# An MoE block's weight splits, all on VectorE, and the gated product's transposes in another PSUM bank

## The chip, the cores and the metric

The kernel runs on one core of one Trainium2 chip. The metric is the device time of one execution in microseconds; where several executions were timed, their median. The engines are named as in the profile: PE is TensorE, with its weight loads as PEld; DVE is VectorE; ACT is ScalarE; POOL is GpSimd; SP is SyncE, which here only issues transfers. In the text they are also called TensorE, Vector, Scalar, Pool and SyncE.

## The reference

Three layers run over 512 tokens of width 1024 (and 256 context tokens in the first). Two of them mix attention, a Fourier and a long-convolution branch and have a convolutional feed-forward. The third is a dilated and a neighbourhood attention, followed by a mixture of experts and a last norm. The change lies in the mixture of experts alone:

```python
def hierarchical_moe(x, w_group, b_group, w_router, b_router, w_gate, w_up, w_down):
    '''Top-1 expert group, then top-2 SwiGLU experts inside it. x: (B,S,D).'''
    ...
    gate = jnp.einsum('nd,edf->nef', xf, w_gate)
    up = jnp.einsum('nd,edf->nef', xf, w_up)
    act = jax.nn.silu(gate) * up * combine[:, :, None].astype(x.dtype)
    out = jnp.einsum('nef,efd->nd', act, w_down)
    return out.reshape(B, S, D).astype(x.dtype)
```

There are 16 experts of width 256, and each of the 512 tokens goes to two of them.

## The kernel before

**Splits.** All data are float32. A matrix product is made of three products of fp32r parts: each operand is split into a high part (a copy in fp32r) and a low part (the original less the high part). `mm3` (lines 296 to 299) issues the three, high by high (L297), high by low (L298) and low by high (L299). For weights Scalar makes the high part (L2035) and Vector or Pool the low part (L2036), both in `wconv`. Both work on chunks of 128x1024.

**The routing** (`route`, from line 1863) sorts the tokens into tiles of 128 rows. Tiles 0 to 15 belong to one expert each, at places known when the kernel is written. Tiles 16, 17 and 18 hold the rows that did not fit; which expert's weights they need is known only on the chip, so their weights are gathered. If more are needed, a conditional part follows (four more tiles); it is not taken here.

**The tiles** run in the order 0 to 9, 16, 17, 18, 10 to 15 (`K.order`). By order of running they are counted 0 to 18 below where that is said. One tile, in `moe` (from line 2053), is:

- `load`: a gather of the tile's 128 rows (xg), issued on Pool two tiles ahead;
- `rows`: eight transposes of xg on TensorE into two PSUM banks (xgp, tag T), each split by Scalar and Vector (xgt, L327 and L328);
- `up`: 24 products of 128x512 from chunks 0 to 3 of the weights (gups), then silu on Scalar (L2080) and the gated product on Vector (ma, L2081);
- `act`: two transposes of ma on TensorE (mat, L2087) and their split (mas, L327 and L328). The bank of mat has the tag T, so it takes turns with the two of xgp;
- `down`: 12 products from chunks 4 and 5 (mdps), copied out by Scalar or Vector (yt) and stored from Scalar's queue. The last two tiles to run are kept in SBUF (yf) and scattered by a product with a matrix of zeros and ones (S).

`down` of a tile is issued behind `up` of the next one. After the fifth tile `scatter_from` builds S (fo, L1786, and its transposes fsp).

**The weights' stream.** `wstream` keeps 18 chunks (three tiles) loaded or under way: `wnext` takes a chunk, splits it and asks for the one 18 further on. Static chunks are loaded from SyncE's queue (L2015), gathered ones from Pool's (L2017). They go by turns into nine buffers called raw and into pages called rawp. A load waits until the splits of the buffer's earlier chunk are done, and the loads of a queue go in order.

**Which splits go to Pool.** `wnext` passes a flag: for static tiles, chunk 2 and chunk 5 (chunk 2 alone in the last tile, tile 15). These are 31 of the 118 splits that `wconv` makes (114 for the 19 tiles, four for the output projection ahead of the routing). Tiles 16 to 18 have all their splits on Vector.

**Order.** The instructions are ordered on each engine by a planner when the kernel is built. A semaphore wait holds up everything behind it on its engine.

**PSUM in this stage**: two banks each for the tags b (mdps), T (xgp, mat, fsp) and g (gups), one for r (the routing's logits and weights, rtp and rwsl) and one for r2.

Of the kernel before, what the change touches and what calls it, by code (L numbers as in the profile page):

```python
# [9 lines left out]
F32 = mybir.dt.float32  # L10
# [4 lines left out]
ALU = mybir.AluOpType  # L15
# [238 lines left out]
class Kern:  # L254
# [1485 lines left out]
    def second_tail(K, mix, xs):  # L1740
        nc, A = K.nc, K.A
# [15 lines left out]
            nc.scalar.dma_start(y[n * 128:n * 128 + 1, :], z)  # L1757
        lt = K.bank([128, 4, 20], name="rtp", tag="r")
        K.phase("wout2")
        ws = [K.wconv(t, False) for t in K.w2raw]  # L1760
        ro = K.branch_norm(1)
        K.wstream(5)
        for tb in range(4):
# [9 lines left out]
        T = {}  # L1773
# [44 lines left out]
        for tb in range(4):  # L1818
            t = ts[2 * tb + 1][0]
# [4 lines left out]
            for h in range(2):  # L1824
                ps = K.bank([128, 512], name="fsc", tag=("T", "g", "b", "T")[tb])
                c = slice(h * 512, h * 512 + 512)
# [6 lines left out]
        for tb in range(4):  # L1833
            ss = K.sm([128, 1], "fss")
            K.sumsq(xs[tb], ss)
            r = K.rsqrt(ss, 1, 1.0 / D, EPS, "fr")
# [188 lines left out]
            K.wq.append((c, j, K.wraw(j, c)))  # L2025
            K.wn += 1

    def wconv(K, raw, pool, pg=False):
        nc = K.nc
        if pg:  # L2030
            hi, lo = K.pg([128, 1024], F32R, "whx"), K.pg([128, 1024], F32R, "wlx")
        else:
            hi = K.wp.tile([128, 1024], F32R, tag="whi", name="whi", bufs=K.NW)
            lo = K.wp.tile([128, 1024], F32R, tag="wlo", name="wlo", bufs=K.NW)
        nc.scalar.activation(hi, raw, AF.Copy)  # L2035
        (nc.gpsimd if pool else nc.vector).tensor_tensor(lo, raw, hi.bitcast(F32), op=ALU.subtract)  # L2036
        return hi, lo

    def wnext(K, j, cs):
        out = []  # L2040
        for c in cs:
            c_, j_, raw = K.wq.popleft()
            assert (c_, j_) == (c, j)
            out.append(K.wconv(raw, j < 16 and c == (2 if j == K.order[-1] else 2 + 3 * (c > 3)), c > 3))
            K.wstream(K.WDEPTH)
        return out

# [5 lines left out]
    def moe(K, tiles, xnd, idx, wsl, weights=None, fin=(), T=None, mid=None, rest=None):  # L2053

        nc, A = K.nc, K.A
        if not weights:
            def weights(j, cs):
                return [K.wconv(K.wraw(j, c), False) for c in cs]

        def load(j):  # L2060
            x = K.page(j, "xg")
            nc.gpsimd.indirect_dma_start(out=x, out_offset=None, in_=xnd,
                                         in_offset=bass.IndirectOffsetOnAxis(ap=idx[:, j:j + 1], axis=0))
            return x

        def rows(x):
            t = [K.page(tiles[0], f"xgt{p}", F32R).rearrange("p (k n) -> p k n", n=128) for p in range(2)]
            for h in range(2):
                ps = K.bank([128, 4, 128], name="xgp", tag="T")
                for k in range(4):  # L2070
                    nc.tensor.transpose(ps[:, k], x[:, (4 * h + k) * 128:(4 * h + k) * 128 + 128], K.ident)  # L2071
                K.split(t[0][:, 4 * h:4 * h + 4], t[1][:, 4 * h:4 * h + 4], ps)
            return t

        def up(j, t, w):
            ps = K.bank([128, 512], name="gups", tag="g")
            for k in range(8):
                K.mm3(ps, (t[0][:, k], t[1][:, k]), (w[k // 2][0][:, k % 2], w[k // 2][1][:, k % 2]), k == 0, k == 7)
            a = K.t2([128, 256], "ma") if j < 19 else K.page(j, "ma")[:, 0:256]
            nc.scalar.activation(a, ps[:, 0:256], AF.Silu)  # L2080
            nc.vector.scalar_tensor_tensor(a, a, wsl[:, j:j + 1], ps[:, 256:512], op0=ALU.mult, op1=ALU.mult)  # L2081
            return a

        def act(a):
            pt = K.bank([128, 2, 128], name="mat", tag="T")
            for k in range(2):
                nc.tensor.transpose(pt[:, k], a[:, k * 128:k * 128 + 128], K.ident)  # L2087
            s = K.t2([128, 2, 2, 128], "mas", F32R)
            K.split(s[:, 0], s[:, 1], pt)
            return s  # L2090

        def down(j, s, w):
            if j in fin:
                T[fin.index(j)] = y = [K.pg([128, 1024], F32R, f"yf{p}") for p in range(2)]
            else:
                y = K.page(j, "yt")
            for h in range(2):
                c = slice(h * 512, h * 512 + 512)
                ps = K.bank([128, 512], name="mdps", tag="b")
                for k in range(2):  # L2100
                    K.mm3(ps, (s[:, 0, k], s[:, 1, k]), (w[k][0][:, c], w[k][1][:, c]), k == 0, k == 1)
                if j in fin:
                    K.split(y[0][:, c], y[1][:, c], ps)
                else:
                    K.ev(y[:, c], ps)
            if j not in fin:
                z, r = (0, j - 2 * (j > 15)) if j < 19 else (1, j - 19)
                nc.scalar.dma_start(K.yb[z][r * 128:r * 128 + 128, :], y)

        tiles = list(tiles)  # L2110
        xs = deque(load(j) for j in tiles[:2])
        t = rows(xs.popleft())
        prev = None
        for i, j in enumerate(tiles):
            if i + 2 < len(tiles):
                xs.append(load(tiles[i + 2]))
            w = [K.wk(v, 512) for v in weights(j, range(4))]
            a = up(j, t, w)
            if xs:
                t = rows(xs.popleft())  # L2120
            if prev:
                down(*prev)
            prev = (j, act(a), weights(j, (4, 5)))
            if mid and i == 4:
                mid()
        if rest:
            rest()
        down(*prev)
# [39 lines left out]
```

## Time and profile before

| | |
|---|---|
| median of three runs | 2298.61 us (2293.86 to 2303.5) |
| profiled execution | 2302.42 us, span 2300.6 us |
| PE busy | 2126.4 us, 92% of the span |
| DVE busy | 1472.3 us, 64% |
| ACT busy | 1013.4 us, 44% |
| POOL busy | 353.0 us, 15% |
| mean granted clock | 0.963 |

The shares are means over the whole span. The page's line of busy tenths in 40 slices shows that they differ by stage: in slices 37 to 39 Vector stands at 8 and 9 tenths, the DMA at 8 and 9, and Pool at 4 to 7, where it is at 0 to 3 in every slice before:

```profile
DVE  4644576567677777767558455565565645669895
ACT  3632562364332232236454464333344544347672
POOL 1300000011010000003100010000001112126744
PEclk8999999979999999998999989999999999979998
DMA  8352022723333344434120432333243345369893
```

One slice is 57.5 us; the experts' stage fills the last four to five. A row of the timeline gives the start in us from the span's start, the length in us, the engine, the line in the kernel, the operation, the tiles written and read, the shape, and in brackets how long the engine sat idle before and what ended that.

### The profile page before, as it was taken

What the parts mean: (1) busy time and instruction counts of PE and PEld (TensorE: products, weight loads), DVE (VectorE), ACT (ScalarE), POOL (GpSimd) and SP (SyncE); (2) the same over time, 40 slices, a digit from 0 to 9 for tenths busy, and PEclk for the clock granted to TensorE, in tenths of its full rate; (3) what the DMA queues carried; (4) which work ended last, traced back from release to release, by engine and by line L of the source; (5) the groups of instructions that cost most, each with busy time, mean ns of one, the idle gap of its engine ahead of it and who ended that gap; (6) DMA issues with size and microseconds to landing.
All of it is one profiled execution on the core that took longest, in us unless ns stands there. A gap on an engine that the chain in (4) does not pass through costs nothing. (4 is left out here: it accounts for less than half of the span.)

```text
span 2300.6 us, 30894 instructions
## 1 busy us (share of the span) xinstructions
PE 2126.4 (92%) x11802; PEld 1725.7 (75%) x11802; DVE 1472.3 (64%) x2451; ACT 1013.4 (44%) x1786; POOL 353.0 (15%) x331
## 2 busy tenths in 40 slices
PE   6999998989999999998998989999989998968895
PEld 3777677768888888886876778888867786756673
DVE  4644576567677777767558455565565645669895
ACT  3632562364332232236454464333344544347672
POOL 1300000011010000003100010000001112126744
PEclk8999999979999999998999989999999999979998
DMA  8352022723333344434120432333243345369893
GB/s 334 100 194 81 10 79 103 268 95 106 106 105 125 125 145 160 142 119 147 42 90 18 166 101 83 101 108 94 86 154 90 88 121 172 138 229 352 318 371 121
DMA packets 94394, 321.19 MB, mean 140 GB/s; under 512 B 11262, under 2 KB 12673, under 8 KB 94244
## 3 DMA queue, kind: packets, MB, share of 16 engines
q1 hardware_dynamic: 81472, 280.37, 35.2%
q0 software_dynamic: 10320, 29.89, 4.2%
q10 hardware_dynamic: 2452, 8.92, 1.0%
q8 instruction: 94, 1.54, 0.3%
q14 instruction: 56, 0.46, 0.1%
HBM read 279.39 MB, written 33.46 MB: 136 GB/s over the span
## 5 line engine op out<-in xcount | busy, mean ns | idle before, releaser
L318 DVE TENSOR_TENSOR wlo<-raw,whi 128x1024 fp32r<-128x1024 f32 x200 | 245.4, 1235 | 179.1 <-ACT whi L317 170.0
L317 ACT ACTIVATE whi<-raw 128x1024 fp32r<-128x1024 f32 x200 | 209.9, 1059 | 257.9 <-PE fps L298 194.3
L297 PE MATMUL fps<-h2x,whi 128*128 128x512 f32 x672 | 262.2, 391 | 3.8 <-DVE cvf L702 3.7
L298 PE MATMUL fps<-h2x,whi 128*128 128x512 f32 x672 | 262.5, 391 | 0.0
L299 PE MATMUL fps<-h2x,wlo 128*128 128x512 f32 x672 | 262.0, 391 | 0.0
L1295 DVE TENSOR_TENSOR y<-y,dps 128x512 f32<-128x512 f32 x200 | 134.0, 683 | 108.8 <-PE dps L299 104.1
L1372 POOL TENSOR_TENSOR cvf<-cvf 128x512 f32<-128x512 f32 x66 | 77.1, 1168 | 803.5 <-DVE cvf L702 703.2
L297 PEld LDWEIGHTS fps<-h2x,whi 128*128 128x128 f32 x672 | 126.3, 188 | 31.0 <-ACT whi L317 4.1
L700 ACT ACTIVATE cvf<-fps,cv 128x512 f32<-128x512 f32 (+1 forms) x126 | 87.5, 695 | 139.0 <-PE fps L299 138.9
L299 PEld LDWEIGHTS fps<-h2x,wlo 128*128 128x128 f32 x672 | 126.5, 188 | 27.7 <-issue 1.6
L298 PEld LDWEIGHTS fps<-h2x,whi 128*128 128x128 f32 x672 | 126.7, 188 | 25.8 <-issue 0.4
L298 PE MATMUL dps<-wlo,actx 128*128 128x512 f32 x352 | 137.1, 389 | 0.0
L297 PE MATMUL dps<-whi,actx 128*128 128x512 f32 x352 | 136.6, 390 | 0.3 <-DVE y L1295 0.3
L299 PE MATMUL dps<-whi,actx 128*128 128x512 f32 x352 | 136.6, 389 | 0.0
L420 DVE SCALAR_TENSOR_TENSOR ma<-wm,cs,ma 128x512 f32<-128x512 f32 x140 | 107.7, 814 | 17.4 <-DMA wm<-in_wmod 17.4
L297 PE MATMUL fps<-hx,whi 128*128 128x512 f32 x288 | 113.7, 395 | 0.5 <-ACT v L921 0.5
L299 PE MATMUL fps<-hx,wlo 128*128 128x512 f32 x288 | 113.3, 393 | 0.0
L298 PE MATMUL fps<-hx,whi 128*128 128x512 f32 x288 | 113.2, 393 | 0.0
L701 DVE SCALAR_TENSOR_TENSOR cvf<-fps,cv,cvf 128x511 f32<-128x511 f32 (+1 forms) x126 | 82.5, 655 | 30.2 <-ACT cvf L700 30.0
L297 PE MATMUL fps<-h2c,whi 128*128 128x256 f32 x336 | 96.3, 286 | 4.1 <-ACT cvf L700 4.1
L298 PE MATMUL fps<-h2c,whi 128*128 128x256 f32 x336 | 96.1, 286 | 0.0
L299 PE MATMUL fps<-h2c,wlo 128*128 128x256 f32 x336 | 96.1, 286 | 0.0
(579 smaller groups left out, 5250.3 us busy)
## 6 DMA issues: line engine op xcount, KB each, us to landing
wm<-in_wmod SPq DMA_DIRECT2D x96, 512.0 KB
raw<-in_wup SPq DMA_DIRECT2D x88, 512.0 KB
raw<-in_win SPq DMA_DIRECT2D x52, 512.0 KB
rawp<-in_wexp SPq DMA_DIRECT2D x48, 512.0 KB
raw<-in_wexp SPq DMA_DIRECT2D x48, 512.0 KB
raw<-in_wdown SPq DMA_DIRECT2D x44, 512.0 KB
raw<-in_wout SPq DMA_DIRECT2D x20, 512.0 KB
xd<-xt SPq DMA_DIRECT2D x20, 512.0 KB
```

The source lines that it names most:

```text
L297: mm(out, st[0], mv[0], start=start, stop=False)
L298: mm(out, st[0], mv[1], start=False, stop=False)
L299: K.lastmm = mm(out, st[1], mv[0], start=False, stop=stop)
L317: nc.scalar.activation(hi, raw, AF.Copy)
L318: (nc.gpsimd if pool else nc.vector).tensor_tensor(lo, raw, hi.bitcast(F32), op=ALU.subtract)
L420: o = nc.vector.scalar_tensor_tensor(a, v, c, a, op0=ALU.mult, op1=ALU.add)
L700: nc.scalar.activation(dst, ps, AF.Identity, scale=w[1], bias=w[3])
L701: nc.vector.scalar_tensor_tensor(dst[:, 1:n], ps[:, 0:n - 1], w[0], dst[:, 1:n], op0=ALU.mult, op1=ALU.add)
L1295: nc.vector.tensor_tensor(y[tb][:, c], y[tb][:, c], pss[hf], op=ALU.add)
L1372: nc.gpsimd.tensor_tensor(t[1], t[0], t[1], op=ALU.mult)
```

## The change

- `wconv` loses its flag: every low part of a weight is made on Vector, none on Pool. `wnext` and two other callers follow.
- In `act`, the bank for the transposes of the gated product has the tag r in place of T.

```diff
-        ws = [K.wconv(t, False) for t in K.w2raw]
+        ws = [K.wconv(t) for t in K.w2raw]
...
-    def wconv(K, raw, pool, pg=False):
+    def wconv(K, raw, pg=False):
...
-        (nc.gpsimd if pool else nc.vector).tensor_tensor(lo, raw, hi.bitcast(F32), op=ALU.subtract)
+        nc.vector.tensor_tensor(lo, raw, hi.bitcast(F32), op=ALU.subtract)
...
-            out.append(K.wconv(raw, j < 16 and c == (2 if j == K.order[-1] else 2 + 3 * (c > 3)), c > 3))
+            out.append(K.wconv(raw, c > 3))
...
-                return [K.wconv(K.wraw(j, c), False) for c in cs]
+                return [K.wconv(K.wraw(j, c)) for c in cs]
...
-            pt = K.bank([128, 2, 128], name="mat", tag="T")
+            pt = K.bank([128, 2, 128], name="mat", tag="r")
```

The arithmetic is the same; only the engine and the bank differ.

## Rows read from the trace of the kernel before

**Rows 1.** busy time by stretch: length, engines' busy us, granted clock, DMA share, GB/s.

```profile
core 0: us, PE busy (x) PEld busy (x) DVE busy (x) ACT busy (x) POOL busy (x), PEclk, DMA share, GB/s
2051.00:2072.40 21.40, 18.53 (x77) 14.32 (x76) 14.75 (x16) 15.90 (x22) 11.62 (x6) 0.84 0.76 269
...
2078.45:2089.20 10.75, 9.53 (x46) 7.68 (x46) 10.57 (x10) 8.25 (x11) 6.96 (x3) 1.00 0.98 355
...
2104.60:2126.00 21.40, 17.30 (x80) 13.52 (x78) 18.32 (x18) 12.66 (x19) 12.04 (x6) 0.92 0.86 328
...
2126.00:2163.00 37.00, 30.17 (x137) 23.18 (x138) 31.52 (x29) 23.51 (x32) 31.41 (x21) 0.96 0.85 292
...
2178.00:2234.00 56.00, 51.80 (x243) 40.64 (x242) 50.84 (x52) 42.98 (x59) 23.84 (x11) 1.00 1.03 412
```

**Rows 2.** groups, 1950 to 2301 us: busy us, mean ns | idle before, releasers.

```profile
L2036 DVE TENSOR_TENSOR wlo<-raw,whi 128x1024 fp32r<-128x1024 f32 x38 | 72.0, 1894 | 4.1 <-ACT whi L2035 3.7 <-DMA raw<-in_wexp 0.5
...
L2036 DVE TENSOR_TENSOR wlo<-rawp,whi 128x1024 fp32r<-128x1024 f32 x22 | 42.3, 1924 | 9.5 <-ACT whi L2035 9.5
...
L2036 POOL TENSOR_TENSOR wlo<-rawp,whi 128x1024 fp32r<-128x1024 f32 x16 | 41.2, 2574 | 35.7 <-ACT whi L2035 24.7 <-issue 10.9
...
L1786 DVE TENSOR_TENSOR fo<-moec,fu 128x512 f32<-128x512 f32 x2 | 3.3, 1650 | 0.0
```

**Rows 3.** timeline of one tile: start, length, instruction [idle before].

```profile
2080.33 2.65 POOL L2036 TENSOR_TENSOR wlx<-raw,whx 128x1024 fp32r<-128x1024 f32 x1 [3.62 <-ACT whx L2035]
...
2081.24 2.83 DVE L2036 TENSOR_TENSOR wlo<-rawp,whi 128x1024 fp32r<-128x1024 f32 x1 [0.18 <-ACT whi L2035]
...
2085.52 3.03 DVE L2036 TENSOR_TENSOR wlo<-raw,whi 128x1024 fp32r<-128x1024 f32 x1
...
2088.47 1.28 DVE L328 TENSOR_TENSOR xgt<-xgp,xgt 128x512 fp32r<-128x512 f32 x2
...
2089.20 0.44 PE L2087 MATMUL mat<-ident,ma 128*128 128x128 f32 x2 [1.23 <-DVE xgt L328]
...
2089.40 0.49 PE L299 MATMUL gups<-whi,xgt 128*128 128x512 f32 x1
```

**Rows 4.** timeline, Vector, two splits with no Pool operation beside them.

```profile
2178.60 1.21 DVE L2036 TENSOR_TENSOR wlx<-raw,whx 128x1024 fp32r<-128x1024 f32 x1
...
2179.74 1.21 DVE L2036 TENSOR_TENSOR wlo<-rawp,whi 128x1024 fp32r<-128x1024 f32 x1
```

**Rows 5.** timeline of the stretch of the gathers, Pool and then TensorE.

```profile
2141.12 1.15 POOL L2017 DMA_INDIRECT raw<-in_wexp,rwr  x1 [0.30 <-issue]
...
2159.45 2.35 POOL L2036 TENSOR_TENSOR wlx<-raw,whx 128x1024 fp32r<-128x1024 f32 x1
...
2163.22 0.94 POOL L2017 DMA_INDIRECT rawp<-in_wexp,rwr  x1 [0.30 <-PE mdps L299]
...
2161.85 0.79 PE L298 MATMUL mdps<-wlx,mas 128*128 128x512 f32 x1 [3.22 <-POOL wlx L2036]
```

**Rows 6.** timeline, TensorE, mat of tiles 0, 5, 7, 10, 13, 17 by order.

```profile
2055.27 0.44 PE L2087 MATMUL mat<-ident,ma 128*128 128x128 f32 x2 [0.32 <-DVE ma L2081]
...
2115.24 0.56 PE L2087 MATMUL mat<-ident,ma 128*128 128x128 f32 x2
...
2136.12 0.44 PE L2087 MATMUL mat<-ident,ma 128*128 128x128 f32 x2
...
2176.07 0.44 PE L2087 MATMUL mat<-ident,ma 128*128 128x128 f32 x2 [0.92 <-DVE xgt L328]
...
2207.60 0.44 PE L2087 MATMUL mat<-ident,ma 128*128 128x128 f32 x2
...
2251.68 0.44 PE L2087 MATMUL mat<-ident,ma 128*128 128x128 f32 x2 [1.62 <-DVE xgt L328]
```

**Rows 7.** timeline, Vector's wait for a load, and SyncE's last load of weights.

```profile
2195.00 1.89 DVE L2036 TENSOR_TENSOR wlo<-raw,whi 128x1024 fp32r<-128x1024 f32 x1 [0.47 <-DMA raw<-in_wexp]
...
2226.98 0.33 SPq L2015 DMA_DIRECT2D rawp<-in_wexp  x1
```

## The prediction

> **What bounds the kernel now.** The change lives in the experts' stage, about 2014 to 2265 us of the span. I read the busy time by stretch first [rows 1], then the grouped splits [rows 2], then one tile instruction by instruction [rows 3], then the stretch with the gathered weights [rows 5] and the periods from tile to tile [rows 6].
>
> In a steady tile (2078.45 to 2089.20) Vector is busy 10.57 of 10.75 us, TensorE 9.53, and the transfers have a share of 0.98, where they reach 1.03 at 412 GB/s in the best stretch [rows 1]. Vector sets the pace and the transfers are close behind it. But Vector's time is not all work. A split that has Vector to itself takes 1.21 us and the next one starts 1.14 us after it [rows 4]; beside a split on Pool it takes 2.83 and 3.03 us [rows 3]. The first of these began at 2081.24 and ended at 2084.07; Pool's split had ended at 2082.98. So Vector's split did nothing until Pool's was over, and then took its 1.1 us. Twice in this tile Vector stands behind Pool, for 2.83 - 1.21 = 1.62 and 3.03 - 1.21 = 1.82 us, 3.4 us in all.
>
> TensorE feels it at one place: the gated product's transposes (mat) wait 1.23 us for Vector's low half of the next rows (xgt), which was queued behind the stretched split [rows 3].
>
> Between 2126 and 2163 Pool is the busiest engine, 31.41 of 37.00 us [rows 1]. It issues the 18 gathers of tiles 16 to 18 there and its own splits stand in the same queue: TensorE waited 3.22 us for a split that Pool had started at 2159.45 [rows 5].
>
> **The change part by part: the splits.** It takes 31 splits off Pool (two in each of 15 static tiles, one in the last) and puts them on Vector.
> - Removed from Vector: the waits behind Pool. The two large groups give 38 x (1.894 - 1.21) = 26.0 and 22 x (1.924 - 1.21) = 15.7 us; the two fo of scatter_from are 3.3 us together where Vector's other 512-column operations take half of 1.28, so 2.0 us [rows 2, 3]. Sum 43.7 us.
> - Added to Vector: 31 x 1.14 = 35.3 us [rows 4].
> - Vector gains 8.4 us over the stage. In the steady tile it is 3.44 less 2 x 1.14, so 10.75 - 1.16 = 9.6 us, about where TensorE stands with 9.53.
>
> Against the steady tile's 9.6 stand the transfers: 10.75 x 0.98 / 1.03 = 10.2 us if they never pause [rows 1]. The nearest rows for the new state are tiles 16, 17 and 18, whose six splits all lie on Vector already: 2207.60 - 2176.07 = 31.5 us for three periods, 10.5 each [rows 6] (the first splits of the next static tiles, some of them on Pool, fall in too). I take 10.4 us, between 10.2 and 10.5, and nearer to the tiles that ran.
>
> By stage, on the profiled execution:
> 1. Tiles 0 to 5, from 2055.27 to 2115.24, 60.0 us for five periods [rows 6], with start-up and scatter_from among them. At 10.4 the five would be 52, but both disturbances stay: start-up is a chain behind the routing, and scatter_from is work. Bounds 0 and 8; I take 3, since fo's 2.0 us go and some ten splits gain (43.7 - 35.3) / 31 = 0.27 us each (less what fo counts in that).
> 2. 2115.24 to 2136.12, two periods of 10.44 [rows 6]: nothing.
> 3. 2136.12 to 2176.07, 39.95 us for three periods [rows 6]. Per tile Pool has six gathers and one gather of rows at 0.94 + 0.30 us [rows 5], 8.7 us, and two splits of about 2.57 [rows 2], together 13.8; the period is 13.3. Without the splits Pool needs 8.7 and drops out. At 10.4 the three take 31.2: 8.7 us less.
> 4. Tiles 16 to 18: already on Vector, nothing.
> 5. 2207.60 to 2251.68, 44.1 us for four periods, 11.0 each [rows 6]. At 10.4: 2.5 us.
> 6. The end behind 2251.68 (last down products, the gather of results, the final norm) has its own chain: nothing, between -1 and 1.
>
> Sum 3 + 8.7 + 2.5 = 14.2 us. Now the cap. At 2195.00 Vector waited 0.47 us for a static weight to land [rows 7]: there, early in tile 10, the stock of loaded weights is used up, so up to this point the kernel can be ahead only by what the transfers are ahead. They were idle before it by 21.4 x (1 - 0.76/1.03) = 5.6, 21.4 x (1 - 0.86/1.03) = 3.5 and 37.0 x (1 - 0.85/1.03) = 6.5 us [rows 1], 15.6 in all. The first belongs to a start that hardly moves: 1 us back. The second shrinks with the scatter's stall: 2 to 3. The third came from Pool's late gathers: 5 to 6.5. So 8 to 10.5 us come back before 2195 and stages 1 and 3, worth 11.7 by themselves, are cut to about 10. With stage 5, behind the cap, 12.5; I say 13 us: from 2051 to 2072.4 the granted clock averages 0.84 [rows 1], so part of that stretch ran at the 1.2 GHz level, and fewer stops may leave less of it.
>
> Here a rule speaks against the change. The gathers are issued on Pool, and each of seven per tile now meets more splits of Vector. The row of one that ran beside a split of Vector has 1.15 us, against 0.94 alone [rows 5]: 0.2 x 7 = 1.5 us per tile on an engine with 1.7 us to spare. The Trainium skill (SBUF — State Buffer, Who interferes with whom) says that a Vector instruction with two SBUF inputs contends with a GpSimd instruction that reads SBUF, and that the one that comes second blocks for the whole instruction. For the splits on Pool this trace agrees (1.62 and 1.82 us of standing still); for the gathers the 1.15 us does not look like a full block. By the rule taken in full the sum would be that of the fourth rival.
>
> **The bank.** mat moves from the two banks that the rows' transposes (xgp) rotate through to the bank that the routing used last, idle in this stage. The wait of mat for xgt (1.23 us here) cannot simply vanish: the product that follows, L299 at 2089.40, reads the same xgt half [rows 3]. So TensorE waits there instead, and what is won is at most mat's own 0.44 us per tile, run inside the stall, and an earlier split of mat. One bank now serves mat alone, a tile apart, so it adds no wait. Between 0 and 0.44 x 17 = 7.5 us; I count 0 apart from the sum, as Vector and the transfers set the pace.
>
> **Sum.** 2302.42 - 13 = 2289.4 for the profiled execution; the median of the runs is 3.8 lower, so **2285.6 us**.
>
> **The rivals.**
> - *The transfers bind earlier* (0.2): only half of the idle time comes back, 5 us, and stage 5 gives 2. For it: share 0.98 already in the steady tile. Against it: 0.85 while Pool was late. 2298.6 - 7 = 2291.6.
> - *TensorE is freed as well* (0.16): stalls go, the clock stays up, and mat fills its gap; periods fall towards 9.6 to 10 and all 15.6 us of idle transfers come back, with 5 behind the cap and 2 in the start. 2298.6 - 22 = 2276.6. Against it: tiles 16 to 18 averaged 10.5.
> - *Vector becomes the late feeder* (0.06, slower than before): it has 10.57 - 3.44 + 2.28 = 9.4 us of its own per tile, and the order in its queue puts the added split ahead of xgt and of mat's low half, so that TensorE waits for each in turn. It decides where Vector idles over 2.1 us per tile waiting for Scalar or TensorE, since the mean period is now (2251.68 - 2055.27) / 17 = 11.55 [rows 6]. At 2.8 us of idling the period is 12.2, and 17 x 0.65 = 11 us are lost: 2309.6.
> - *The gathers starve* (0.06): each of seven issues waits out a split of 1.14, so Pool needs 8.7 + 8.0 = 16.7 per tile in stage 3, 3 x 3.4 = 10 us more than now, against stage 1 and 5's 5.5: 2303.
> - *It doesn't do what it says*: Vector's stretched splits were slow for another reason and stay so. Then 35 us are added to a full engine. The end at 2084.07, 1.1 us behind Pool's, leaves it hardly a chance; it is counted within the two before.
>
> **How the numbers follow.** The forecast has 0.52, with 9 to 17 us of gain. About 0.5% (11.5 us) is what a measurement can tell from no change, and the forecast sits just past it: some 0.42 of its 0.52 lies beyond, if the clock and the scatter give a little. With the second rival faster is 0.57; same is the rest of the forecast, the first rival and half of the two slow ones, 0.37; slower 0.06. The range leaves out the slow rivals and the ends of the others: 2275 to 2296.
>
> **What would show it.** All 118 splits in Vector's rows at 1.21 to 1.23 us, none over 1.5 us; Pool without a 128x1024 operation before 2265. No wait of TensorE for Pool. The wait for xgt now stands before L299 and is shorter. From 2126 to 2163 the transfers' share is 0.95 or more, and the three periods of stage 3 are near 31 us. The last weight load leaves about 10 us earlier than at 2227. I am wrong if the periods in stages 3 and 5 stay above 11, or if Vector idles over 2 us per tile.

## The result and the profile after

| | before | after |
|---|---|---|
| median of the runs | 2298.9 us of four (2293.86 to 2303.5) | 2273.93 us of four (2272.35 to 2278.48) |
| ratio | | 0.9894, 95% interval 0.9876 to 0.9913 |
| profiled execution, span | 2302.42, 2300.6 us | 2278.48, 2276.7 us |

The changed kernel is faster by 25 us, 13 were forecast, and the time lies just under the range of 2275 to 2296. First the page's line of 40 slices, rows of the same engines as those shown of before:

```profile
DVE  4634576567677777767658464555665645659986
POOL 1300000001010000002200001000000212101512
DMA  8352022723323344434120433323324334559993
```

In the last four slices Pool's 6 7 4 4 became 1 5 1 2, Vector's 9 8 9 5 became 9 9 8 6 and the DMA's 9 8 9 3 became 9 9 9 3. The groups of splits, 1950 to 2301 us (columns as in [rows 2]; whi and wlo are the high and low parts of chunks 0 to 3, whx and wlx those of chunks 4 and 5):

```profile
L2036 DVE TENSOR_TENSOR wlo<-raw,whi 128x1024 fp32r<-128x1024 f32 x38 | 46.4, 1220 | 1.6 <-ACT whi L2035 1.4
L2036 DVE TENSOR_TENSOR wlo<-rawp,whi 128x1024 fp32r<-128x1024 f32 x38 | 46.4, 1220 | 6.6 <-ACT whi L2035 6.5
L1786 DVE TENSOR_TENSOR fo<-moec,fu 128x512 f32<-128x512 f32 x2 | 1.4, 686 | 0.0
```

A split takes 1220 ns on the mean where it took 1894 and 1924 [rows 2], and the two fo take 1.4 us for 3.3. More splits take less of Vector's time: the 76 of these two groups cost 92.8 us, the 60 of before 114.3. No split of the 118 takes over 1.23 us, where 26 of Vector's 87 took over 1.5 before; each of those 26 ended 1.08 or 1.09 us behind the end of a split on Pool (worked out from the traces).

Below, a tile's end is the end of its last up product (L299 on gups), a period is the time between two such ends, and the stage is the time from the first end to the last, 18 periods. These are worked out from the traces. The first end moves between 2043.7 and 2055.5 us from profile to profile, and between 2048.5 and 2054.5 in three of the changed kernel alone, so stages are compared and not places in the span. In the two profiles here it is 2051.7 and 2051.9. Periods in us, in the order of running:

| | 0 to 5 | 5 to 6 (scatter_from) | 6 to 7 | 7 to 10 | 10 to 13 | 13 to 17 | 17 to 18 | end of the span |
|---|---|---|---|---|---|---|---|---|
| before | 53.7 | 16.3 | 9.8 | 39.0 | 32.5 | 43.0 | 11.2 | 43.5 |
| after | 46.7 | 14.3 | 9.5 | 29.8 | 33.7 | 40.2 | 9.4 | 41.2 |
| gain | 7.0 | 2.0 | 0.3 | 9.3 | -1.2 | 2.7 | 1.8 | 2.3 |

The columns follow the forecast's stages: stage 1 is the first two, then come stages 2 to 5 and the end. (The forecast's marks were the rows of mat. By tile ends the whole period with scatter_from falls to stage 1 and stage 2 is one period, not two.) The gains sum to 24.1 before rounding; with the first end 0.2 later that is the 23.9 us between the spans. Busy time by stretch, columns as in [rows 1]: first the kernel before, from the first end to tile 12's and on to the last, then after in the same way, then three stretches of [rows 1] in the kernel after.

```profile
2051.70:2193.60 141.90, 122.68 (x550) 95.80 (x549) 121.83 (x114) 98.42 (x132) 86.96 (x50) 0.94 0.91 332
2193.60:2257.20 63.60, 57.69 (x273) 45.50 (x273) 57.09 (x53) 45.83 (x63) 34.67 (x15) 1.00 0.74 293
```

```profile
2051.90:2176.80 124.90, 118.23 (x554) 93.70 (x553) 115.08 (x134) 97.56 (x132) 37.28 (x29) 0.99 0.99 383
2176.80:2235.50 58.70, 57.11 (x270) 45.04 (x269) 55.00 (x64) 46.19 (x63) 5.84 (x5) 1.00 0.76 303
...
2051.00:2072.40 21.40, 20.17 (x100) 16.20 (x99) 20.85 (x26) 18.90 (x26) 1.25 (x2) 1.00 0.86 302
2104.60:2126.00 21.40, 20.40 (x97) 16.02 (x98) 19.23 (x23) 16.74 (x23) 8.09 (x6) 1.00 1.02 393
2126.00:2163.00 37.00, 36.46 (x169) 28.73 (x169) 35.93 (x42) 30.89 (x43) 22.33 (x17) 1.00 1.00 379
```

Two things are to be seen. Vector's busy time falls by 6.8 and 2.1 us although it does 31 splits more. And TensorE, busy 122.68 of 141.90 us before, is busy 118.23 of 124.90 and then 57.11 of 58.70 us: behind tile 12, where the transfers have room (0.76), it now sets the pace, 57.11 / 6 = 9.5 us of its own in a period of 9.8. Its granted clock, 0.84 to 0.96 in these stretches before [rows 1], stays at 1.00 (the 2.4 GHz level).

One tile of after (timeline; TensorE's rows, then Vector's), to set beside [rows 3]:

```profile
2208.07 0.38 PE L2087 MATMUL mat<-ident,ma 128*128 128x128 f32 x2
2208.29 1.04 PE L2071 MATMUL xgp<-ident,xg 128*128 128x128 f32 x8
2209.57 0.50 PE L297 MATMUL gups<-whi,xgt 128*128 128x512 f32 x1 [0.25 <-issue]
...
2210.30 0.50 PE L299 MATMUL gups<-whi,xgt 128*128 128x512 f32 x1
```

```profile
2207.51 1.22 DVE L2036 TENSOR_TENSOR wlo<-raw,whi 128x1024 fp32r<-128x1024 f32 x1
2208.90 0.42 DVE L328 TENSOR_TENSOR mas<-mat,mas 128x256 fp32r<-128x256 f32 x1 [0.17 <-ACT mas L327]
2209.55 0.69 DVE L328 TENSOR_TENSOR xgt<-xgp,xgt 128x512 fp32r<-128x512 f32 x1 [0.23 <-issue]
```

Nothing waits over 0.25 us, and mat runs ahead of the row's transposes instead of behind Vector's xgt. TensorE's waits for xgt over the whole stage (waits: total us, times, longest), before and then after:

```profile
PE mat L2087 <- DVE xgt L328: 9.1, 10, 1.6
PE mdps L298 <- POOL wlx L2036: 4.7, 2, 3.2
```

```profile
PE gups L299 <- DVE xgt L328: 0.9, 2, 0.5
```

The wait for xgt moved from mat to L299, as forecast, and shrank from 9.1 us (and 2.1 that stood before L299) to 0.9; no wait of TensorE for Pool is left. The last weight load leaves SyncE at 2208.91, where it was 2226.98 [rows 7]: 18 us earlier, where about 10 were forecast.

One wait is new and long, in the period from tile 11 to 12 (timeline of TensorE; then the stretches before and behind it):

```profile
2164.36 0.38 PE L2087 MATMUL mat<-ident,ma 128*128 128x128 f32 x2
2166.66 1.33 PE L2071 MATMUL xgp<-ident,xg 128*128 128x128 f32 x8 [1.93 <-DMA xg<-xnd,ridx]
```

```profile
2158.00:2164.74 6.74, 6.74 (x31) 5.35 (x29) 6.74 (x7) 5.10 (x6) 0.18 (x1) 1.00 1.03 419
2166.66:2170.70 4.04, 4.04 (x14) 3.03 (x15) 2.60 (x4) 3.37 (x5) 0.00 (x0) 0.58 1.03 410
```

TensorE stood 1.93 us for the gathered rows of a tile, which come behind the gathered weights, and then worked 4.04 us at 0.58, most of them at the 1.2 GHz level. By the clock alone these 4.04 us were 0.58 x 4.04 = 2.3 us of work, so the stop cost up to 1.93 + 1.7 us. The period is 14.6 us, where it was 12.0 before and those beside it are 10.1 and 9.0. In e6 below, with stops of 1.54 and 0.25 us here and the clock at 1.00 all through, it is 13.2: by that the fall of the clock cost some 1.3 us. Not every stop brings such a fall: in e14 below one of 2.40 us at this place was followed by none.

### The profile page after: what moved, and what is told of

It reads as the page before. It is cut to its first block, busy times and chain, and to the rows that moved or that the text cites. A ratio compares the mean times of both kernels' runs of the same rounds, so it can differ in the third digit from the quotient of the medians.

```text
span 2276.7 us, 30881 instructions
## 1 busy us (share of the span) xinstructions
PE 2120.3 (93%) x11802; PEld 1721.1 (76%) x11802; DVE 1463.2 (64%) x2482; ACT 1013.3 (45%) x1786; POOL 271.5 (12%) x300
## 3 DMA queue, kind: packets, MB, share of 16 engines
q8 instruction: 94, 1.54, 0.3%
## 5 line engine op out<-in xcount | busy, mean ns | idle before, releaser
L299 PE MATMUL fps<-h2x,wlo 128*128 128x512 f32 x672 | 262.5, 391 | 0.0
L299 PEld LDWEIGHTS fps<-h2x,wlo 128*128 128x128 f32 x672 | 126.9, 189 | 27.9 <-issue 1.6
L299 PE MATMUL dps<-whi,actx 128*128 128x512 f32 x352 | 136.6, 389 | 0.0
L299 PE MATMUL fps<-hx,wlo 128*128 128x512 f32 x288 | 113.2, 393 | 0.0
L701 DVE SCALAR_TENSOR_TENSOR cvf<-fps,cv,cvf 128x511 f32<-128x511 f32 (+1 forms) x126 | 82.5, 655 | 30.1 <-ACT cvf L700 30.1
L299 PE MATMUL fps<-h2c,wlo 128*128 128x256 f32 x336 | 95.8, 285 | 0.0
```

Source lines behind the costliest of these rows:

```text
L299: K.lastmm = mm(out, st[1], mv[0], start=False, stop=stop)
L701: nc.vector.scalar_tensor_tensor(dst[:, 1:n], ps[:, 0:n - 1], w[0], dst[:, 1:n], op0=ALU.mult, op1=ALU.add)
```

## The experiments

**1. Each part alone.** e1 is the changed kernel with mat back in tag T; e2 is the kernel before with mat in tag r.

```diff
 e1:  -            pt = K.bank([128, 2, 128], name="mat", tag="r")
      +            pt = K.bank([128, 2, 128], name="mat", tag="T")
 e2:  the kernel before, with the last line of the change alone
```

> The splits go to Vector, the bank of mat stays T. Theory A (the 25 us are the waits behind Pool, in Vector's queue and in Pool's own): 17 to 25 us under the kernel before, and no split of Vector over 1.3 us. Theory B (the bank is what was under-counted: mat no longer waits for xgt, and TensorE's order can change): 10 to 14 us under before, as the prediction's sum had it for the splits, with mat's wait for xgt still in the list of waits.

> Only the bank of mat moves to r, Pool keeps its 31 splits. Theory A: 0 to 4 us under before, since TensorE then waits for xgt at the next product; Vector's stretched splits stay (2.4 to 3.8 us each). Theory B: 8 to 13 us under before.

e1: 2270.76 us, ratio 0.9883 (0.9857 to 0.991). e2: 2305.04 us, ratio 1.003 (1.0015 to 1.0046). The splits carry the whole gain, more than theory A's 17 to 25 us, and the bank alone costs 0.3%. With mat in T as before, e1's wait of mat for xgt is 0.2 us: it is the moved splits that end it, not the bank. Busy time of e1 in the two parts of the stage, then TensorE's wait in e2:

```profile
2043.70:2163.60 119.90, 114.85 (x549) 91.19 (x548) 114.13 (x134) 96.75 (x132) 34.87 (x29) 1.00 0.99 394
2163.60:2223.00 59.40, 57.90 (x274) 45.51 (x273) 54.77 (x64) 44.73 (x63) 6.72 (x6) 1.00 0.78 312
```

```profile
PE gups L299 <- DVE xgt L328: 14.6, 11, 2.3
```

In e2 the wait for Vector's xgt is not gone but stands before L299, 14.6 us where mat's was 9.1 and L299's 2.1: moving mat out of the way of a late Vector brings nothing. That it loses 7 us was foreseen by neither theory; the planner orders TensorE's work differently with the other bank, and no run here separates that from the wait.

**2. Is Vector's added work paid for?** e3 is the changed kernel without the 31 low parts that used to lie on Pool; the high part stands in their place, so 35 us of Vector's work are left out.

```diff
+        if skip:
+            hi = K.pg([128, 1024], F32R, "whx") if pg else K.wp.tile([128, 1024], F32R, tag="whi", name="whi", bufs=K.NW)
+            nc.scalar.activation(hi, raw, AF.Copy)
+            return hi, hi
```

> The changed kernel, but the 31 low parts that used to be Pool's are left out altogether (the high part is used in their place, so these products are not the reference's). It takes 35 us of Vector's work away. Theory A with TensorE as the next bound: within 5 us of the changed kernel, so about 2270 us. Theory C (Vector is the bound after the change, at 9.4 of about 10 us per tile): 10 us or more under the changed kernel, about 2262 us.

2270.32 us, ratio 0.9864 (0.9833 to 0.9894), and a stage of 182.4 us against 183.6 in the changed kernel. 35 us of Vector's work are worth about 1 us of the stage: they lie beside TensorE's work. The clearest place is from tile 13 to 17, where the transfers have room: 40.3 us without this work, 40.2 with it. The rival of the late Vector falls.

**3. Why did a split stand still?** e5 is the changed kernel with Pool repeating its 31 subtractions into a tile that nobody reads; in e6 Pool writes instead, two memsets for each.

```diff
 e5:  +            nc.gpsimd.tensor_tensor(idle, raw, hi.bitcast(F32), op=ALU.subtract)
 e6:  +            nc.gpsimd.memset(idle, 0.0)
      +            nc.gpsimd.memset(idle, 1.0)
```

> The changed kernel, and Pool does its 31 subtractions again beside Vector's, into a tile that nobody reads. So Vector has all 118 splits and Pool holds up what it held up before. Theory A (a Pool operation that reads SBUF keeps Vector's splits standing still): the stretched splits of 2.4 to 3.8 us are back, Vector's load per tile is 9.4 + 3.4 = 12.8 us, and the stage of 184 us grows by some 16 x 2.8 = 45 us; 2300 to 2325 us in all. Rival (the stretched splits had another cause, and only Pool's late results cost time): no stretched split, within 5 us of the changed kernel.

> The same, but Pool only writes: two memsets of 128x1024 in place of each subtraction. Pool's queue is held up for a like time, and no SBUF is read. Theory A: no split over 1.3 us and within 4 us of the changed kernel. Rival (any Pool operation of that length disturbs, by its queue or by its writing): as slow as the one that reads, 2300 us or more.

e5: 2331.42 us, ratio 1.0136 (1.0116 to 1.0157), above theory A's 2300 to 2325. e6: 2278.02 us, ratio 0.9902 (0.9881 to 0.9924). Timeline of Vector and Pool in e5, its group of splits, then the timeline of e6:

```profile
2087.66 1.23 DVE L2036 TENSOR_TENSOR wlx<-raw,whx 128x1024 fp32r<-128x1024 f32 x1 [0.43 <-ACT whx L2035]
2087.76 3.34 POOL L2039 TENSOR_TENSOR idle<-raw,whx 128x1024 bf16<-128x1024 f32 x1 [3.95 <-DVE wlx L2036]
2088.80 3.38 DVE L2036 TENSOR_TENSOR wlo<-raw,whi 128x1024 fp32r<-128x1024 f32 x1
...
L2036 DVE TENSOR_TENSOR wlo<-rawp,whi 128x1024 fp32r<-128x1024 f32 x38 | 66.3, 1744 | 7.6 <-ACT whi L2035 7.3
```

```profile
2075.53 0.95 POOL L2040 MEMSET idle<- 128x1024 bf16 x1
2075.74 1.21 DVE L2036 TENSOR_TENSOR wlo<-raw,whi 128x1024 fp32r<-128x1024 f32 x1
```

In e5 Vector's split from 2088.80 ends at 2092.18, 1.08 us behind the end of Pool's subtraction (2091.10): the same picture as in the kernel before [rows 3]. It goes both ways: this subtraction of Pool began 0.10 us after a split of Vector and took 3.34 us, where the one at 2093.04 takes 2.52. In e6 the split beside a write of Pool keeps to 1.21 us, the 26 that met a memset for 0.2 us or more stay under 1.23 us, and the means of the groups stay at 1217 to 1224 ns. So it is Pool's reading that stops Vector. The Trainium skill (SBUF — State Buffer, Who interferes with whom) has this rule, and e5 and e6 agree with it. One limit: the memsets wait for nothing and ran early, 2024.6 to 2100.2, so e6 tells of the splits beside them, and its time says nothing on a Pool that is busy through the whole stage. And e5's 57 us over the changed kernel are not Vector's stretching alone (some 50 us by its four groups, part of it beside TensorE's work): Pool's reads also hold the buffers, and Scalar waits 13.9 us for them in seven waits, and the mean granted clock is 0.954 where the changed kernel has 0.966. What each is worth was not taken apart.

**4. Stage 3 alone.** The forecast put 8.7 of its 14.2 us on tiles 7 to 9. e4 is the kernel before with only those tiles' splits moved to Vector.

```diff
-            out.append(K.wconv(raw, j < 16 and c == (2 if j == K.order[-1] else 2 + 3 * (c > 3)), c > 3))
+            out.append(K.wconv(raw, j < 16 and c == (2 if j == K.order[-1] else 2 + 3 * (c > 3)) and j not in (7, 8, 9), c > 3))
```

> The kernel before, but tiles 7, 8 and 9, beside whose splits the gathered weights are issued, have all six splits on Vector. If Pool's queue in the stretch of the gathers is the largest single part, 6 to 10 us under before, and the two long periods of 14 us there fall to about 10. If the transfers had held that stretch, under 3 us.

2297.0 us, ratio 0.9985 (0.9967 to 1.0003): not clear of no change, and not the 6 to 10 us. The two long periods went, 14.2 and 14.6 to 10.1 and 10.0, 8.7 us, just the forecast's number. But the next two grew from 11.0 and 12.0 to 14.5 and 17.8, 9.3 us. Busy time of e4 from tile 0 to 5, 5 to 8 and 8 to 12, then TensorE's rows in the grown periods:

```profile
2046.90:2098.50 51.60, 45.41 (x216) 35.74 (x215) 47.57 (x43) 40.73 (x54) 32.64 (x15) 1.00 0.92 348
2098.50:2135.40 36.90, 32.85 (x147) 26.00 (x146) 32.68 (x34) 24.97 (x34) 21.66 (x12) 0.91 0.82 301
2135.40:2187.80 52.40, 43.33 (x189) 34.29 (x189) 38.77 (x45) 32.41 (x44) 22.79 (x19) 0.90 0.99 386
...
2161.46 1.62 PE L2071 MATMUL xgp<-ident,xg 128*128 128x128 f32 x8 [3.26 <-DMA xg<-xnd,ridx]
2177.97 1.94 PE L2071 MATMUL xgp<-ident,xg 128*128 128x128 f32 x8 [5.30 <-DMA xg<-xnd,ridx]
```

The transfers stand at 0.99 and 386 GB/s in the last of these stretches, and TensorE waits 3.26 and 5.30 us for gathered rows: the tiles arrive sooner than their data. In e1, where the gain of stage 3 stands, the tiles ahead keep the transfers moving as well (394 GB/s up to tile 12); in e4 they are at 348 and 301 GB/s. That this is the reason is argued, not shown.

**5. Are the rows late, or is the stock used up?** In e10 (e4) and e11 (e1) the rows are gathered three tiles ahead in place of two.

```diff
-        xs = deque(load(j) for j in tiles[:2])
+        xs = deque(load(j) for j in tiles[:3])
...
-            if i + 2 < len(tiles):
-                xs.append(load(tiles[i + 2]))
+            if i + 3 < len(tiles):
+                xs.append(load(tiles[i + 3]))
```

> The kernel before with all splits of tiles 7, 8 and 9 on Vector, as in the earlier run that won 9 us there and lost them at the next two tiles, and now each tile's rows are gathered three tiles ahead in place of two. Theory F (the loss was the gather of rows standing behind 18 gathered weights in Pool's transfers, 17 to 19 us from issue to use): periods 10 and 11 of that run, 14.4 and 17.9 us, fall to 10 to 12, and the time to 6 to 12 us under before. Theory G (the loss is the stock of weights that is used up, whatever the rows do): the long periods stay, 2 to 4 us under before.

> All splits on Vector, mat in T, and the rows gathered three tiles ahead. Theory F: 0 to 4 us under the splits alone, whose long period there is only 10.9 us. If the extra page for the rows holds up the weights' stream, as much slower.

e10: 2300.89 us, ratio 1.0004 (0.9988 to 1.002). e11: 2283.63 us, ratio 0.9944 (0.9927 to 0.9962), 13 us slower than e1. Neither theory's time came. In e10 the period from 10 to 11 falls to 9.8 us, but the one from 11 to 12 is 19.7, and 12.2 and 15.1 follow. Two rows of e10's timeline:

```profile
2171.77 1.94 PE L2071 MATMUL xgp<-ident,xg 128*128 128x128 f32 x8 [4.33 <-DMA xg<-xnd,ridx]
2174.21 1.06 ACT L2035 ACTIVATE whi<-rawp 128x1024 fp32r<-128x1024 f32 x1 [7.71 <-DMA rawp<-in_wexp,rwr]
```

Asked for a tile earlier in the program, the late rows left Pool only 1.4 us earlier in the span (at 2157.92, in e4 at 2159.28), and they are still late by 4.33 us, so e10 doesn't try theory F cleanly. But just behind them Scalar has to wait 7.71 us for gathered weights: the weights are late as well, so the order of the rows alone isn't the cause. (In e4 the two late gathers of rows were used 11.6 and 18.7 us after their issue, not 17 to 19.) In e11 the period from 11 to 12 is 18.2 us, Scalar waits 6.43 us for gathered weights in it, and later periods of 11.7, 10.8 and 14.6 follow. The additional rows stand in a page of the kind that the weights use (xg and rawp share them), so that they take room from the weights' stream, in e10 too, is likely, but not shown.

**6. Do the transfers bind?** In e7 (e1) and e8 (the kernel before) chunk 5 is not loaded; it is taken from chunk 4's buffer, a sixth of the loads less.

```diff
-            K.wq.append((c, j, K.wraw(j, c)))
+            K.wq.append((c, j, K.wq5 if c == 5 else K.wraw(j, c)))
+            K.wq5 = K.wq[-1][2]
```

> Splits alone on Vector, and a sixth of the weights is not loaded: chunk 5 of each tile is split from the buffer of chunk 4 (so the down products are not the reference's). All splits and products stay. Theory D (with the splits moved, the transfers, at 1.03 of share and 403 to 414 GB/s up to tile 12 by order, hold those tiles): the stretch from the first tile to the thirteenth, 119.9 us, falls by 4 to 8 us, and the whole by 4 to 10 against the splits alone. Theory E (TensorE's 9.5 to 10 us per tile is the bound there too): within 3 us of the splits alone.

> The kernel before with chunk 5 taken from the buffer of chunk 4 in the same way, Pool's splits as they were. If the transfers had capped the kernel before about tile 12, as the prediction put it, some 5 us or more under before. If the waits behind Pool set its pace and the transfers had room (332 GB/s up to there, against 413 at best), within 3 us of before.

e7: 2269.98 us, ratio 0.9868 (0.9846 to 0.9891). e8: 2293.57 us, ratio 0.9975 (0.9963 to 0.9988). Busy time from tile 0 to 12, e7, then e8:

```profile
2048.60:2169.60 121.00, 113.39 (x545) 91.61 (x544) 113.55 (x134) 98.61 (x132) 39.60 (x26) 0.99 0.92 344
```

```profile
2047.60:2184.80 137.20, 119.39 (x549) 93.80 (x548) 122.71 (x114) 98.75 (x132) 87.21 (x47) 0.96 0.82 300
```

With the splits moved, fewer loads bring nothing up to tile 12 (121.0 us against e1's 119.9). Tile by tile it is two things: the three periods from tile 7 to 10 fall from 10.0 to 10.3 us each to 9.3 and 9.4, so the loads do hold these by some 0.8 us each, and then the one from 11 to 12 is 13.9 in place of 10.9, with a wait of 2.81 us for rows. In the kernel before, fewer loads bring 5.4 us of the stage and 0.25% of the time, which is the size that was expected if the transfers capped it. But e8 doesn't show that: 2.0 us of it are the first period, where the clock stayed up (below); 5.1 lie in tiles 7 to 10, where three of the 18 gathers also left Pool's queue; and tiles 10 to 13 give 2.1 back. The transfers and Pool's issuing are not told apart there.

**7. Is TensorE held by its banks?** e9 is e1 with three banks for T, the routing's two tags sharing one.

```diff
-        R = K.bank([128, 96], name="rank", tag="r2")
+        R = K.bank([128, 96], name="rank", tag="r")
...
-        pi = K.bank([128, 24], name="ridx", tag="r2")
+        pi = K.bank([128, 24], name="ridx", tag="r")
...
-... K.psum(b=2, T=2, g=2, r=1, r2=1):
+... K.psum(b=2, T=3, g=2, r=1):
```

> Splits on Vector; the routing's two banks become one, and the bank that this frees is a third for tag T, which the rows' transposes and mat share again. If TensorE's waits for xgt are worth what they show (mat and the products after it wait 6 to 10 us in all), 3 to 8 us under the splits alone (2270.8); if TensorE's 10.05 us per tile is its own work and the hand-over from the transposes to their split, within 4 us of it.

2272.36 us, ratio 0.9892 (0.9867 to 0.9916). Behind tile 13 periods of 9.85 where e1 has 10.0 to 10.1, but 15.0 from tile 11 to 12, with a wait of 2.71 us for rows: no gain in all. What is left of the period there is TensorE's own work: from tile 12 to 17 it is busy 49.12 of 49.28 us.

**8. Bank r against T beside the moved splits.** Three more runs: the changed kernel twice (e12, e14) and e1 once (e13), the last two timed together.

```diff
 e12, e14: the changed kernel
 e13:      e1
```

> The changed kernel once more, beside the others on one chip: 23 to 27 us under before. If the bank of mat costs something with the splits on Vector, as it did without, 2 to 6 us over the splits alone (ratio 0.9883); if not, the same.

> The splits alone on Vector, mat in T, timed beside the changed kernel in the same rounds. If the bank costs something with the splits moved, 26 to 30 us under before, and 4 to 7 us under the changed kernel beside it. If it costs nothing, both within 3 us of each other.

> The changed kernel in the same rounds. If the bank costs something, 20 to 24 us under before; if it costs nothing, 25 to 28 us as the splits alone.

e12: 2279.34 us, ratio 0.9918 (0.9898 to 0.9937). e13: 2270.48 us, 0.9885 (0.9861 to 0.9908). e14: 2274.04 us, 0.9896 (0.9875 to 0.9918). e12 is slower than expected (20.5 us under before, not 23 to 27). The medians of e13 and e14 differ by 3.6 us and their intervals overlap, so whether the bank costs anything beside the moved splits stays open. The stages point to a cost: 183.6, 183.6 and 183.0 us with r, 179.3 and 180.7 with T. With r two periods are longer (scatter_from 14.3 against 12.3; from 11 to 12 14.0 to 14.6 against 10.9) and the first is shorter (8.4 against 10.1). The splits alone, 2270.5 to 2270.8 us, are the fastest form that ran here and no slower than the change as a whole.

## Why the forecast was too small

- **The mechanism held.** Vector stood still behind Pool's reads (e5, e6); freed of them, its added work costs next to nothing (e3). Forecast: Vector's busy time 8.4 us less over the stage; measured 8.8 (6.75 and 2.09). All groups of its splits stand at 1218 to 1225 ns.
- **The step that failed is the size of the gain ahead of tile 12**: stage 1 at 3 us, and the cap that lets only "8 to 10.5 us come back before 2195". Up to the end of tile 12 the kernel gained 141.9 - 124.9 = 17.0 us. Had stage 1 been sized right, the cap would still have cut it away.
- **The cap** took its room from the DMA's busy share and let half to two thirds of it come back. Both were short. By the share up to tile 12, some 17 us of idle time before are some 5 after, so about 12 came back. The other 5 that the kernel gained were no idle time: a packet, 3.65 KB on the mean in each, took 160 ns before, 151 after and 145 in the stretch of 412 GB/s (worked out from the traces), so the share counted slow packets as full use. By bytes, the kernel before moved 332 GB/s x 141.9 us = 47.1 MB up to tile 12, which at the 412 GB/s of [rows 1] take 114.3 us: 27.6 us of room, where the share over the same stretch gives 141.9 x (1 - 0.91 / 1.03) = 16.5. The kernel after moves 47.8 MB there in 124.9 us, which leaves 8.9 us of room. The thought behind the cap, that being ahead of the transfers is worth nothing, fits e4; its size was wrong.
- **Stage 1 was sized at 3; it gave 9.0** (7.0, and 2.0 in scatter_from). The sum had 9.6 us for a tile without the stops and then set 10.4 in its place, because the transfers need 10.2 for a tile's bytes. But with 18 chunks loaded ahead and room in the transfers the first five periods ran at 8.4 to 10.3 us, 9.3 on the mean: below that floor, so it doesn't bind while the stock lasts. "A start that hardly moves" was wrong with it.
- **Stage 2**: 0 forecast, 0.3 measured. **Stage 3**: 8.7 and 9.3, the best term of the sum, though no gain of stage 3 alone: taken by itself it is paid back at once (e4). **Stage 4**: 0 and -1.2, the wait for gathered rows, a new one. **Stage 5**: 2.5 and 2.7; its periods became 10.0 to 10.1, not 10.4, but those of before were 10.75 by tile ends, not 11.0, and the two errors cancel.
- **The end was sized at 0** (-1 to 1) and gave 4.0: the last period fell from 11.2 to 9.4, and what lies behind it from 43.5 to 41.2. In the other kernels the latter takes 39.1 to 41.5 us without Pool's splits and 41.2 to 45.5 with them; that the last tile's split on Pool is the reason is argued, not shown.
- **The bank was counted 0**, within 0 to 7.5 us of gain. Alone it costs 0.3% (e2): a loss was not bounded. That the wait would move to L299 was right.
- **The clock** was counted at some half a microsecond, which was too little. From 2051 to 2072.4 it is 1.00 for 0.84, up to tile 12 0.99 for 0.94. Of the 17.0 us up to there 12.5 are waits of TensorE that went (141.90 - 122.68 = 19.2 us idle to 6.7); the other 4.5 are its busy time for nearly the same products, which the clock would explain for the most part (argued, not shown). One place can be taken apart. In the first period of the kernel before and of e4, which has Pool's splits there too, the same product waits as long (before, then e4):

```profile
2058.99 0.79 PE L299 MATMUL gups<-whi,xgt 128*128 128x512 f32 x1 [2.07 <-DVE xgt L328]
2059.58 0.63 PE L297 MATMUL gups<-whi,xgt 128*128 128x512 f32 x1
```

```profile
2054.20 0.50 PE L299 MATMUL gups<-whi,xgt 128*128 128x512 f32 x1 [2.09 <-DVE xgt L328]
2054.53 0.40 PE L297 MATMUL gups<-whi,xgt 128*128 128x512 f32 x1
```

  The products that follow come 0.43 us apart before and 0.23 in e4, where the clock stays at 1.00, and the period is 11.9 us before and 9.8 in e4. So 2.1 of stage 1's 9.0 us are the clock, and the wait alone doesn't say whether it falls.

So the 13 us become 24.1: 6.0 from stage 1, 4.0 from the end, 1.7 that the cap had cut from stages 1 and 3, 0.6 from stage 3, 0.3 from stage 2 and 0.2 from stage 5, less 1.2 in stage 4 and the half for the clock, which is in stage 1.

- **The rivals.** The one that came is "TensorE is freed as well" (2276.6, with 0.16). It needed all of the idle transfer time back, which by bytes there was. The row held against it, 10.5 us a tile for tiles 16 to 18, was one of the old state: in e1 the three periods from 10 to 13 take 30.1 us, 10.0 each. "The transfers bind earlier" falls with the bytes. The late Vector falls with e3, and "it doesn't do what it says" with the 118 splits at 1.22 us. The starving gathers were right in kind and wrong in size: a gather that starts beside a split does stand (a split on Vector and two gathers on Pool, in the kernel after):

```profile
2140.10 1.22 DVE L2036 TENSOR_TENSOR wlx<-raw,whx 128x1024 fp32r<-128x1024 f32 x1
2140.16 1.97 POOL L2062 DMA_INDIRECT xg<-xnd,ridx  x1 [0.30 <-issue]
...
2146.23 0.94 POOL L2017 DMA_INDIRECT raw<-in_wexp,rwr  x1 [0.30 <-issue]
```

  The gather at 2140.16 began 0.06 us after a split and took 1.03 us more than the one at 2146.23, which met no split of a weight. So the 1.15 us of [rows 5] need not be the price of a meeting: that gather began 0.34 us before the end of a split and may have met only its end. But not every gather meets a split so: the 37 gathers of this stage average 1.25 us after and 1.33 before (worked out from the trace), and Pool, rid of its splits, is busy 22.33 of 37 us where it was 31.41 [rows 1].

## What to carry to other kernels

Work given to Pool to relieve Vector can cost Vector more than it takes off it when both read SBUF: compare one operation's time beside Pool's with its time alone before counting a relief. Size the room in the transfers by bytes over the best rate that the trace shows, not by the busy share, and apply a transfers' floor only from where the stock of loaded data is used up. A stage that is sped up alone may only wait for its data one tile later, as in e4, so try the stages ahead of it together with it. Before a gain is put down to one cause, compare the granted clock of the two profiles in that stretch.

## What the hardware showed beyond that

- The busy share of the DMA engines is no measure of capacity: 0.91 at 332 GB/s, 0.92 at 348, 0.99 at 383 to 394, 1.03 at 410 to 419 in this stage; and e7 has 0.92 at 344 with a sixth of the loads left out. From 0.91 to 1.03 the share grows by 13%, the rate by 24%.
- 31 useless subtractions on a Pool that else had only gathers to issue cost 57 us (e5 over the changed kernel), some 1.8 us each, though no product needs their result.
- A stop of 1.93 us of TensorE was followed by 4.04 us at 0.58 of the clock, which cost another 1.3 (against e6) to 1.7 us (by the clock alone). Stops as long or longer were followed by no fall in other profiles: 2.09 us in e4's first period, 2.40 in e14.
